# The recurrence's tables in one order for both heads of a pair: corrections in the first 64 rows, values in the last 64

## The chip, the cores and the metric

The kernel runs on one core of one Trainium2 chip. The metric is the device time of one execution in microseconds, taken as the median of several runs.

## What is computed

Two layers of a hybrid trunk over 512 latent and 256 context tokens of width 1024. Each layer projects its normalised input, runs three mixers (differential attention, a two-directional RWKV-7 recurrence, a short convolution), merges them, and ends with a mixture of 16 experts. The change touches the recurrence alone, 8 heads of width 64 in two directions:

```python
def step(s, inp):
    wt, kkt, at, kt, vt = inp[:5]
    sa = jnp.einsum('bhvk,bhk->bhv', s, kkt)
    s = s * wt[:, :, None, :] - sa[..., None] * (kkt * at)[:, :, None, :] + vt[..., None] * kt[:, :, None, :]
    y = jnp.einsum('bhvk,bhk->bhv', s, inp[5]) if emit else None
    return s, y
```

A step decays the state `s`, takes a correction `sa` along the removal key, and adds value times key. The last layer emits nothing for context tokens.

## The kernel before

The recurrence is cut into 12 chunks of 64 tokens (`NCH`), and the 8 heads into 4 pairs, one pair on the 128 partitions: head 0 on rows 0 to 63, head 1 on rows 64 to 127. Both directions stand in the free dimension. So a layer has 48 chain steps, and the kernel 96.

For a chunk, `window` makes what does not depend on the state: decayed keys `kc` (L683, L684) and decayed receptance and removal keys `kr` (L674, L676), their products on TensorE in a bank `slot`, masked by `scc` into `sc` (L700) and `sv` (L701), the keys turned to token order (`tok`, L708), and the inverse of a unit triangular matrix, built in six levels (`nb` L715, `wt` L725, `xt`, `xx`). It is a generator of nine parts. `ahead` advances the windows of the next three chunks by three parts each before a chain step is recorded, so a window is begun three steps ahead and done one step ahead.

`chain` makes what depends on the state: `V` holds the state and the chunk's values; TensorE multiplies it with `sv`, the right-hand side `zr` (L803 to L807) is solved with the inverse, the first solution `sa` (L813) is refined once, the result goes into `V` (L822, L824) and is copied once more to `sa` (L827) where the window emits; the next state is the product with `tok` plus the scaled old state `sf` (L776), added into the next `V` (L844), and the output rows are copied to `y` (L853).

The two heads keep opposite orders. Head 0 has its own corrections and state in rows 0 to 63 and its values in rows 64 to 127, head 1 the other way round:

```python
hs, ho = slice(64 * h, 64 * h + 64), slice(64 - 64 * h, 128 - 64 * h)
v.tensor_tensor(g.sc[hs, :, :nm, hs], ps[hs, :, h, :nm], self.scc[hs, :, :nm], ALU.mult)
v.tensor_tensor(g.sv[ho, :, :nm, h], ps[ho, :, h, :nm], self.scc[ho, :, :nm], ALU.mult)
```

Each instruction on these tables is therefore written once per head, on 64 partitions.

A planner decides when dense work fills in: the input projections and adaLN pieces (`pw`, `pa`) are handed out in small units, a fixed amount per chain step (`fills`: 6.0 per step in the first layer, 3.0 in the second). Weights come by SP's queue; ScalarE rounds them (`w_hi`, L132) and GpSimd takes the rest (`w_lo`, L134). A scheduler orders each engine's instructions when the program is built, by priorities (chain above preparation above windows above dense products). Every engine runs its queue in that order.

Of the kernel before, what the change touches and what calls it, by code (L numbers as in the profile page):

```python
# [8 lines left out]
F32 = mybir.dt.float32  # L9
# [58 lines left out]
class Trunk:  # L68
# [429 lines left out]
    def pair(self, p, full):  # L498
# [48 lines left out]
        def rows(s):  # L547

            self.need(q.u["value"])
            b0, nb = SEGB[s]  # L550
            vt = q.vt[s] = rp.tile([P, 2 * nb, HD], F32, name="vt", tag=f"vt{s}")
            self.requarter(q.v[:, b0 * P:], nb, lambda c, h: vt[64 - 64 * h:128 - 64 * h, c::2])

        def rates(s):

# [4 lines left out]
            if s == 0:  # L560
                q.f = rp.tile([P, 2, NCH], F32, name="f", tag="f", bufs=2)
                q.lm = rp.tile([P, 2, NCH], F32, name="lm", tag="lm")
            nc.gpsimd.memset(D[:, 0, :, 0:1], 0.0)
            nc.gpsimd.memset(D[:, 1, :, 64:65], 0.0)
            for d in range(2):
# [27 lines left out]
            x = slice(max(n0 - 1, 0), n0 + nch - 1)  # L593
            nc.gpsimd.tensor_tensor(q.f[:, :, x], q.f[:, :, x], q.lm[:, :, x.start + 1:x.stop + 1], ALU.add)
            nc.scalar.activation(q.f[:, :, x], q.f[:, :, x], AF.Exp, scale=S_DEC)

        def bonus(s):
            b0, nb = SEGB[s]
# [37 lines left out]
    def window(self, q, n, emit, kb):  # L636
# [28 lines left out]
        t2 = rp.tile(shp, F32, name="t2", tag="t2")  # L665
        pl.tensor_tensor(t2, th, at(e3, True), ALU.mult)


        kc, kr, g.sc = kb
        if emit:  # L670
            self.need(q.u["receptance"])
        for h in range(2):
            hs = slice(64 * h, 64 * h + 64)
            pl.tensor_tensor(kr[hs, :, h, 0], kk[hs], at(e, False)[hs], ALU.mult)  # L674
            if emit:
                pl.tensor_tensor(kr[hs, :, h, 1], two(q.r)[hs], at(e, True)[hs], ALU.mult)  # L676
        yield

        nm = 2 if emit else 1
        g.sv = rp.tile([P, 2, 2, 2, 64], F32, name="sv", tag="sv", bufs=4)  # L680
        for h in range(2):
            hs, ho = slice(64 * h, 64 * h + 64), slice(64 - 64 * h, 128 - 64 * h)
            v.tensor_tensor(kc[hs, :, ho], two(q.k)[hs], t1[hs], ALU.mult)  # L683
            v.tensor_tensor(kc[hs, :, hs], kk[hs], t2[hs], ALU.mult)  # L684
            dst = g.sv[hs, :, :nm, h]
            if n:
                f = q.f[hs, :, n - 1, None, None].to_broadcast([64, 2, nm, 64])
                pl.tensor_tensor(dst, kr[hs, :, h, :nm], f, ALU.mult)
            else:
                pl.tensor_copy(dst, kr[hs, :, h, :nm])  # L690
        yield

        bank = self.slots[n % 3]
        ps = bank.rearrange("p (d h m i) -> p d h m i", d=2, h=2, m=2)
        self.mark()
        for d in range(2):
            self.mm(ps[:, d, :, :nm], kc[:, d], kr[:, d, :, :nm], True, True)
        for h in range(2):
            hs, ho = slice(64 * h, 64 * h + 64), slice(64 - 64 * h, 128 - 64 * h)
            v.tensor_tensor(g.sc[hs, :, :nm, hs], ps[hs, :, h, :nm], self.scc[hs, :, :nm], ALU.mult)  # L700
            v.tensor_tensor(g.sv[ho, :, :nm, h], ps[ho, :, h, :nm], self.scc[ho, :, :nm], ALU.mult)  # L701
        if n < NCH - 1:

            g.tok = rp.tile([P, 2, P], F32, name="tok", tag="tok", bufs=4)
# [6 lines left out]
        i3 = n % 3  # L711
        mat = lambda n_, dt=F16, tag=None, bufs=1: rp.tile([P, 2, P], dt, name=n_, tag=tag or f"{n_}{i3}", bufs=bufs)
        prod = lambda j=0: bank[:, 256 * j:256 * j + 256].rearrange("p (d x) -> p d x", d=2)
        nb = mat("nb")
        nc.gpsimd.tensor_tensor(  # L715
            nb, g.sc[:, :, 0], self.ident[:, None].to_broadcast([P, 2, P]), ALU.add
        )
        x = xt = None
        for l in range(6):
            ps = prod()  # L720
            self.mark()
            for d in range(2):
                self.mm(ps[:, d], nb[:, d], self.ident16 if l == 0 else x[:, d], True, True)
            wt = mat("wt")
            v.tensor_tensor(wt, ps, self.lvm[:, :, l], ALU.mult)  # L725
            if l == 0:
                x = wt
                xt = mat("xt")
                v.tensor_tensor(xt, nb, self.lvm[:, ::-1, 0], ALU.mult)
                yield  # L730
                continue
            ps = prod()
            self.mark()
            for d in range(2):
                self.mm(ps[:, d], wt[:, d], xt[:, d], True, True)
            if l < 5:
                ps2 = prod(1)
                self.mark()
                for d in range(2):
                    self.mm(ps2[:, d], xt[:, d], wt[:, d], True, True)  # L740
                x = mat("xx")
                nc.scalar.activation(x, ps2, AF.Copy)  # L742
                xt = mat("xt")
            else:
                xt = mat("xtr", F32R, "xtr", 4)
            nc.scalar.activation(xt, ps, AF.Copy)
            if l < 5:
                yield
        g.xt = xt

    def value_rows(self, q, n):

        t = self.rp.tile([P, 2, 2, HD], F32, name="V", tag="V", bufs=3)
        s, z0, z1, _ = seg_chunks(n)
        for h in range(2):
            ho = slice(64 - 64 * h, 128 - 64 * h)
            self.nc.gpsimd.tensor_copy(t[ho, :, h], self.two(q.vt[s][ho], z0, z1))
        return t

    def chain(self, q, n, V, emit):  # L760
# [1 line left out]
        nc, rp, tc = self.nc, self.rp, self.tc  # L762
        v = nc.vector
        g = q.win.pop(n)
        halves = [slice(0, 64), slice(64, 128)]
        if n == 0:
            V = self.value_rows(q, 0)
            for h, hs in enumerate(halves):
                nc.gpsimd.memset(V[hs, :, h], 0.0)
        last = n == NCH - 1  # L770
        out = None if last else self.value_rows(q, n + 1)
        if n and not last:
            sf = rp.tile([P, 2, HD], F32, name="sf", tag="sf")
            fc = q.f[:, :, n - 1]
            for h, hs in enumerate(halves):
                nc.gpsimd.tensor_tensor(  # L776
                    sf[hs], V[hs, :, h], fc[hs, :, None].to_broadcast([64, 2, HD]), ALU.mult
                )


        own = list(enumerate(halves))
        both = lambda t, d: t[:, d, None].to_broadcast([P, 2, HD])
        pz = self.psz.tile([P, 512], F32, name="pz", tag="z")
        zz = pz[:, 0:256].rearrange("p (d h x) -> p d h x", d=2, h=2)
        aa = pz[:, 256:384].rearrange("p (d x) -> p d x", d=2)
# [9 lines left out]

        self.mark()
        begin(zz, lambda d: g.sv[:, d, 0])
        sa = first = None
        for it in range(2):
            r = rp.tile([P, 2, HD], F32R, name="zr", tag="zr", bufs=2)  # L800
            for h, hs in own:
                if it:
                    v.tensor_tensor(r[hs], zz[hs, :, h], sa[hs], ALU.subtract)  # L803
                elif h:
                    v.tensor_copy(r[hs], zz[hs, :, h])
                else:
                    nc.scalar.activation(r[hs], zz[hs, :, h], AF.Copy)  # L807
            self.mark()
            for d in range(2):
                self.mma(aa[:, d], g.xt[:, d], r[:, d])  # L810
            if not it:
                sa = rp.tile([P, 2, HD], F32, name="sa", tag="sa", bufs=2)
                nc.scalar.activation(sa, aa, AF.Copy)  # L813
                self.mark()
                for d in range(2):
                    self.mma(zz[:, d], g.sc[:, d, 0], both(sa, d))
                if emit:

                    first = begin(yy, lambda d: g.sv[:, d, 1])
        for h, hs in own:  # L820
            if h:
                nc.scalar.activation(V[hs, :, h], aa[hs], AF.Copy)  # L822
            else:
                v.tensor_copy(V[hs, :, h], aa[hs])  # L824
        if emit:
            sa = rp.tile([P, 2, HD], F32, name="sa", tag="sa", bufs=2)
            nc.scalar.activation(sa, aa, AF.Copy)  # L827
        self.mark()
        tok = lambda d: g.tok[:, d]
        if last:  # L830
# [5 lines left out]
        else:  # L836
            begin(pss, tok)
        if emit:
            for d in range(2):
                self.mma(yy[:, d], g.sc[:, d, 1], both(sa, d))  # L840
        if not last:
            for h, hs in own:
                if n:
                    v.tensor_tensor(out[hs, :, h], pss[hs, :, h], sf[hs], ALU.add)  # L844
                else:
                    v.tensor_copy(out[hs, :, h], pss[hs, :, h])
        if emit:
            s, z0, z1, nch = seg_chunks(n)
            if n % 4 == 0 and n < 8:
# [40 lines left out]
    def rwkv_phase(self, full):  # L890
        nc, tc = self.nc, self.tc
        with ExitStack() as st:
# [2 lines left out]
            self.slots = [psrw.tile([P, 512], F32, name=f"slot{j}") for j in range(3)]  # L895
            self.psmm = st.enter_context(tc.tile_pool(reuse_waits="tile", name="psmm", bufs=1, space=PSUM))
            self.psz = st.enter_context(tc.tile_pool(reuse_waits="tile", name="psz", bufs=1, space=PSUM))
            kc, kr, sc = (
                [self.rp.tile(shape, F32, name=f"{n}{a}") for a in range(m)]
                for n, m, shape in (("kc", 2, [P, 2, P]), ("kr", 2, [P, 2, 2, 2, 64]), ("sc", 4, [P, 2, 2, P]))  # L900
            )
            for t in kr + sc:
                nc.gpsimd.memset(t, 0.0)
            self.mm_bufs, self.fl_tag = {"mm": 1, "fl": 2}, "fl"
            self.units, self.raws, self.ws, self.due = [], [], [], 0.0
# [36 lines left out]
            def ahead(n, steps):  # L942

                for j in range(max(steps)):
                    for a, m in enumerate(steps):
# [1 line left out]
                        if j >= m or n + a >= 4 * NCH:  # L947
                            continue
                        if n + a not in gens:
                            gens[n + a] = self.window(q, c, full or c >= 4, (kc[c % 2], kr[c % 2], sc[(n + a) % 4]))  # L950
                        do(lambda: next(gens[n + a], None))

            call = lambda f, *a: (lambda: f(*a))
# [984 lines left out]
```

## Time and profile before

| what | value |
|---|---|
| median of 3 runs | 3648.34 us (3643.23 to 3650.91) |
| the profiled execution, its time | 3643.64 us |
| its span | 3641.9 us |
| first recurrence, about | 110 to 830 us |
| second recurrence, about | 2110 to 2760 us |

In the profile PE is TensorE's products, PEld its weight loads, DVE VectorE, ACT ScalarE, POOL GpSimd. L81, L85 and L108 are helpers that issue TensorE's instructions, so those are told apart by their tiles. A wait names the instruction that stood idle, then the one that ended it.

### The profile page before, as it was taken

The page shows a single profiled execution, that of the slowest core. Times are in us where ns is not written, and L with a number is a line of the kernel's source. Part 1 is how long each engine was busy: PE and PEld are TensorE (multiplying, and loading weights), DVE is VectorE, ACT ScalarE, POOL GpSimd, SP SyncE. Part 2 cuts the span into 40 slices and gives each one's busy share as a digit, 9 for nine tenths or more (in the row PEclk, how much of TensorE's full clock was granted, in tenths as well). Part 3 has the DMA queues.
Part 4 walks back from the last instruction along what each step waited for, and adds up shares of the span by engine and source line. Part 5 has one row for each costly group of instructions (what it writes and reads, how often), then busy time and mean ns, then how long its engine had stood idle before and what let it go on. Part 6 is the DMA issues. An engine that isn't in the chain of part 4 may idle for free.

```text
span 3641.9 us, 56218 instructions
## 1 busy us (share of the span) xinstructions
PE 3367.1 (92%) x20863; PEld 2243.8 (62%) x20863; DVE 1950.3 (54%) x4725; ACT 1289.5 (35%) x3233; POOL 1133.7 (31%) x1729
## 2 busy tenths in 40 slices
PE   6999999999998989999999898888899989799998
PEld 3777777777987882233333477676678968543342
DVE  6687878764665461121222577878864665412122
ACT  3354555543454211111111345555553542211111
POOL 3555465543320410000000255656554303100000
PEclk9999999999998989999999899999999989899999
DMA  5323132334106336778888410111113154499998
GB/s 182 101 67 98 35 110 67 123 120 144 47 33 222 121 123 253 288 294 327 328 319 335 153 57 29 36 37 39 36 51 101 36 177 157 186 409 409 409 409 350
DMA packets 297045, 620.94 MB, mean 171 GB/s; under 512 B 19258, under 2 KB 160532, under 8 KB 296772
## 3 DMA queue, kind: packets, MB, share of 16 engines
q1 hardware_dynamic: 293028, 605.30, 46.0%
q0 software_dynamic: 1728, 6.29, 0.5%
q10 hardware_dynamic: 2016, 5.77, 0.4%
q8 instruction: 165, 2.70, 0.3%
q14 instruction: 108, 0.88, 0.1%
HBM read 584.00 MB, written 33.29 MB: 170 GB/s over the span
## 4 chain that ended last, share of the span: by engine, by line
PE 50%; DVE 9%; DMA 2%; ACT 2%; issue 2%; POOL 1%; DVEq 0%; ACTq 0%; POOLq 0%
PE ph L81 13%; PE pw L81 6%; PE py L81 6%; PE pc L81 4%; PE po L81 3%; PE slot L81 2%; PE pt L81 2%; PE psc L81 2%; PE pyc L81 2%; PE ba L81 2%; PE pz L85 2%; DMA we<-in_exp_w 2%; PE py L85 1%; PE pxi L81 1%; DVE wt L725 1%
## 5 line engine op out<-in xcount | busy, mean ns | idle before, releaser
L81 PE MATMUL ph<-we,xin 128*64 128x512 f32 x2048 | 513.3, 605 | 5.4 <-DVE hid L1721 2.8
L81 PE MATMUL pw<-hhi,w_hi 128*128 128x512 f32 (+1 forms) x1272 | 490.7, 390 | 15.0 <-ACT w_hi L132 6.7
L81 PE MATMUL pw<-hlo,w_hi 128*128 128x512 f32 (+1 forms) x1272 | 451.2, 359 | 0.0
L81 PE MATMUL pw<-hhi,w_lo 128*128 128x512 f32 (+1 forms) x1272 | 450.9, 360 | 0.3 <-POOL w_lo L134 0.3
L134 POOL TENSOR_TENSOR w_lo<-w_raw,w_hi 128x1024 fp32r<-128x1024 f32 x124 | 300.5, 2429 | 357.2 <-ACT w_hi L132 296.8
L81 PEld LDWEIGHTS ph<-we,xin 128*64 128x64 f32 x2048 | 151.0, 139 | 325.8 <-issue 315.2
L1793 POOL TENSOR_TENSOR ylo<-y,yhi 128x512 fp32r<-128x512 f32 x28 | 35.2, 1281 | 889.3 <-ACT yhi L1792 889.3
L725 DVE TENSOR_TENSOR wt<-slot,lvm 128x256 f16<-128x256 f32 x576 | 230.3, 418 | 94.0 <-PE slot L81 66.1
L81 PEld LDWEIGHTS pw<-hhi,w_hi 128*128 128x128 f32 x1272 | 243.6, 193 | 45.0 <-ACT w_hi L132 8.0
L81 PEld LDWEIGHTS pw<-hhi,w_lo 128*128 128x128 f32 x1272 | 242.1, 192 | 36.1 <-issue 2.6
L81 PEld LDWEIGHTS pw<-hlo,w_hi 128*128 128x128 f32 x1272 | 244.5, 193 | 30.6 <-issue 12.3
L132 ACT ACTIVATE w_hi<-w_raw 128x1024 fp32r<-128x1024 f32 x168 | 177.0, 1057 | 239.7 <-DMA w_raw<-in_w_in 77.8
L81 PE MATMUL py<-we,hT 128*64 128x512 f32 x1024 | 249.3, 607 | 8.3 <-DMA we<-in_exp_w 3.0
L742 ACT ACTIVATE xx<-slot 128x256 f16<-128x256 f32 x384 | 145.9, 382 | 162.8 <-PE slot L81 137.5
L1720 ACT ACTIVATE sl<-ph 64x512 f32<-64x512 f32 x64 | 37.8, 591 | 449.4 <-PE ph L81 429.7
L1803 DVE TENSOR_TENSOR xr<-xr,psc 128x512 f32<-128x512 f32 x144 | 90.4, 681 | 195.5 <-PE psc L81 195.4
L1721 DVE TENSOR_TENSOR hid<-sl,ph 64x512 f32<-64x512 f32 x64 | 44.1, 690 | 268.3 <-ACT sl L1720 267.9
L81 PEld LDWEIGHTS py<-we,hT 128*64 128x64 f32 x1024 | 70.3, 138 | 153.0 <-issue 134.4
L81 PE MATMUL pt<-w_hi,hhi 128*128 128x256 f32 x544 | 155.8, 288 | 5.4 <-ACT xk L1117 2.0
L81 PE MATMUL pt<-w_lo,hhi 128*128 128x256 f32 x544 | 155.5, 286 | 3.4 <-POOL w_lo L134 3.4
L81 PE MATMUL pt<-w_hi,hlo 128*128 128x256 f32 x544 | 154.7, 285 | 0.0
L81 PE MATMUL slot<-xt,wt 128*128 128x128 f16 x960 | 132.2, 224 | 21.6 <-DVE wt L725 21.1
(412 smaller groups left out, 7661.9 us busy)
## 6 DMA issues: line engine op xcount, KB each, us to landing
we<-in_exp_w SPq DMA_DIRECT2D x384, 1024.0 KB
w_raw<-in_w_in SPq DMA_DIRECT2D x124, 512.0 KB
ada_w<-in_ada_w SPq DMA_DIRECT2D x96, 512.0 KB
w_raw<-in_w_branch SPq DMA_DIRECT2D x24, 512.0 KB
w_raw<-in_w_out SPq DMA_DIRECT2D x20, 512.0 KB
gd<-gt SPq DMA_DIRECT2D x24, 384.0 KB
g<-gd SPq DMA_DIRECT2D x24, 384.0 KB
gd<-gt SPq DMA_DIRECT2D x24, 256.0 KB
```

Source lines behind the costliest of these rows:

```text
L81: return self.leg(self.nc.tensor.matmul(out, lhsT, rhs, start=start, stop=stop))
L85: return self.leg(self.nc.tensor.matmul(out, lhsT, rhs, start=start, stop=True, skip_group_check=True))
L132: nc.scalar.activation(hi, raw, AF.Copy)
L134: self.lo_eng.tensor_tensor(lo, raw, hi.bitcast(F32), ALU.subtract)
L725: v.tensor_tensor(wt, ps, self.lvm[:, :, l], ALU.mult)
L742: nc.scalar.activation(x, ps2, AF.Copy)
L1720: nc.scalar.activation(sl, ph[0:64, ns], AF.Silu)
L1721: v.tensor_tensor(hid[0:64, ns], sl, ph[64:128, ns], ALU.mult)
L1793: (v if by_block else self.ylo_eng[nh]).tensor_tensor(lo, yn, hi.bitcast(F32), ALU.subtract)
L1803: v.tensor_tensor(x, x, pt, ALU.add)
```

## The change

Both heads now keep one order: corrections, state and solutions of both heads in rows 0 to 63, with the head in the free dimension, and keys and values in rows 64 to 127. One mask product per window writes `sc` for both heads; GpSimd copies its lower half into the lower half of `sv`. `kc` is written by two products of 128 rows. `nb` is written by two half-height additions into a fixed table whose other blocks were zeroed once. The first solution is evicted by two half-height ScalarE instructions into rows 0 to 63 of a fixed table `x1` whose lower half is zero; the copy of the last solution is gone, and the output's second product takes `V`. `sf` is one GpSimd product with a copy `fs` of the decays. The value rows `vt` are evicted whole, and `value_rows` copies them by direction instead of by head. `sv`, `nb` and `x1` are fixed tables; `sc` comes from a pool of 4; the pool of `xtr` has 3 buffers for 4.

```diff
@@ -548,8 +548,11 @@
 
             self.need(q.u["value"])
             b0, nb = SEGB[s]
-            vt = q.vt[s] = rp.tile([P, 2 * nb, HD], F32, name="vt", tag=f"vt{s}")
-            self.requarter(q.v[:, b0 * P:], nb, lambda c, h: vt[64 - 64 * h:128 - 64 * h, c::2])
+            vt = q.vt[s] = rp.tile([P, nb, 2, HD], F32, name="vt", tag=f"vt{s}")
+            pt = self.bank().rearrange("p (b t) -> p b t", t=P)
+            for b in range(nb):
+                self.tr(pt[:, b], q.v[:, (b0 + b) * P:(b0 + b + 1) * P])
+            nc.scalar.activation(vt.rearrange("p b h x -> p b (h x)"), pt[:, :nb], AF.Copy)
 
         def rates(s):
 
@@ -560,6 +563,7 @@
...
+                q.fs = rp.tile([64, 2, 2, NCH], F32, name="fs", tag="fs", bufs=2)
...
+            for h in range(2):
+                nc.gpsimd.tensor_copy(q.fs[:, h, :, x], q.f[64 * h:64 * h + 64, :, x])
...
-        kc, kr, g.sc = kb
+        kc, kr, g.sv, nb = kb
         if emit:
             self.need(q.u["receptance"])
         for h in range(2):
             hs = slice(64 * h, 64 * h + 64)
-            pl.tensor_tensor(kr[hs, :, h, 0], kk[hs], at(e, False)[hs], ALU.mult)
+            pl.tensor_tensor(kr[hs, :, 0, h], kk[hs], at(e, False)[hs], ALU.mult)
             if emit:
-                pl.tensor_tensor(kr[hs, :, h, 1], two(q.r)[hs], at(e, True)[hs], ALU.mult)
+                pl.tensor_tensor(kr[hs, :, 1, h], two(q.r)[hs], at(e, True)[hs], ALU.mult)
         yield
 
         nm = 2 if emit else 1
-        g.sv = rp.tile([P, 2, 2, 2, 64], F32, name="sv", tag="sv", bufs=4)
+        v.tensor_tensor(kc[:, :, 64:128], two(q.k), t1, ALU.mult)
+        v.tensor_tensor(kc[:, :, 0:64], kk, t2, ALU.mult)
         for h in range(2):
-            hs, ho = slice(64 * h, 64 * h + 64), slice(64 - 64 * h, 128 - 64 * h)
-            v.tensor_tensor(kc[hs, :, ho], two(q.k)[hs], t1[hs], ALU.mult)
-            v.tensor_tensor(kc[hs, :, hs], kk[hs], t2[hs], ALU.mult)
-            dst = g.sv[hs, :, :nm, h]
+            hs = slice(64 * h, 64 * h + 64)
+            dst = g.sv[0:64, :, :nm, h]
             if n:
                 f = q.f[hs, :, n - 1, None, None].to_broadcast([64, 2, nm, 64])
-                pl.tensor_tensor(dst, kr[hs, :, h, :nm], f, ALU.mult)
+                pl.tensor_tensor(dst, kr[hs, :, :nm, h], f, ALU.mult)
             else:
-                pl.tensor_copy(dst, kr[hs, :, h, :nm])
+                pl.tensor_copy(dst, kr[hs, :, :nm, h])
         yield
 
+        g.sc = rp.tile([P, 2, 2, 2, 64], F32, name="sc", tag="sc", bufs=4)
         bank = self.slots[n % 3]
-        ps = bank.rearrange("p (d h m i) -> p d h m i", d=2, h=2, m=2)
+        ps = bank.rearrange("p (d m h i) -> p d m h i", d=2, h=2, m=2)
         self.mark()
         for d in range(2):
-            self.mm(ps[:, d, :, :nm], kc[:, d], kr[:, d, :, :nm], True, True)
-        for h in range(2):
-            hs, ho = slice(64 * h, 64 * h + 64), slice(64 - 64 * h, 128 - 64 * h)
-            v.tensor_tensor(g.sc[hs, :, :nm, hs], ps[hs, :, h, :nm], self.scc[hs, :, :nm], ALU.mult)
-            v.tensor_tensor(g.sv[ho, :, :nm, h], ps[ho, :, h, :nm], self.scc[ho, :, :nm], ALU.mult)
+            self.mm(ps[:, d, :nm], kc[:, d], kr[:, d, :nm], True, True)
+        if emit:
+            fl = lambda t: t.rearrange("p d m h i -> p (d m) h i")
+            mask = self.scc.rearrange("p d m i -> p (d m) i")[:, :, None].to_broadcast([P, 4, 2, 64])
+            v.tensor_tensor(fl(g.sc), fl(ps), mask, ALU.mult)
+        else:
+            mask = self.scc[:, :, 0, None].to_broadcast([P, 2, 2, 64])
+            v.tensor_tensor(g.sc[:, :, 0], ps[:, :, 0], mask, ALU.mult)
+        pl.tensor_copy(g.sv[64:128, :, 0], g.sc[64:128, :, 0])
...
-        nb = mat("nb")
-        nc.gpsimd.tensor_tensor(
-            nb, g.sc[:, :, 0], self.ident[:, None].to_broadcast([P, 2, P]), ALU.add
-        )
+        for h in range(2):
+            hs = slice(64 * h, 64 * h + 64)
+            pl.tensor_tensor(
+                nb[hs, :, hs], g.sc[0:64, :, 0, h], self.ident[0:64, None, 0:64].to_broadcast([64, 2, 64]), ALU.add
+            )
...
     def chain(self, q, n, V, emit):
@@ -762,24 +772,19 @@
         nc, rp, tc = self.nc, self.rp, self.tc
         v = nc.vector
         g = q.win.pop(n)
-        halves = [slice(0, 64), slice(64, 128)]
+        lo = slice(0, 64)
         if n == 0:
             V = self.value_rows(q, 0)
-            for h, hs in enumerate(halves):
-                nc.gpsimd.memset(V[hs, :, h], 0.0)
+            nc.gpsimd.memset(V[lo], 0.0)
         last = n == NCH - 1
         out = None if last else self.value_rows(q, n + 1)
         if n and not last:
-            sf = rp.tile([P, 2, HD], F32, name="sf", tag="sf")
-            fc = q.f[:, :, n - 1]
-            for h, hs in enumerate(halves):
-                nc.gpsimd.tensor_tensor(
-                    sf[hs], V[hs, :, h], fc[hs, :, None].to_broadcast([64, 2, HD]), ALU.mult
-                )
-
-
-        own = list(enumerate(halves))
-        both = lambda t, d: t[:, d, None].to_broadcast([P, 2, HD])
+            sf = rp.tile([64, 2, 2, HD], F32, name="sf", tag="sf")
+            f = q.fs[:, :, :, n - 1].rearrange("p h d -> p d h")[:, :, :, None].to_broadcast([64, 2, 2, HD])
+            nc.gpsimd.tensor_tensor(sf, V[lo], f, ALU.mult)
+
+
+        own = [(0, slice(0, 64)), (1, slice(64, 128))]
...
@@ -795,12 +800,13 @@
 
         self.mark()
         begin(zz, lambda d: g.sv[:, d, 0])
-        sa = first = None
+        x1 = self.x1[n % 2]
+        first = None
         for it in range(2):
             r = rp.tile([P, 2, HD], F32R, name="zr", tag="zr", bufs=2)
             for h, hs in own:
                 if it:
-                    v.tensor_tensor(r[hs], zz[hs, :, h], sa[hs], ALU.subtract)
+                    v.tensor_tensor(r[hs], zz[hs, :, h], x1[lo, :, h], ALU.subtract)
                 elif h:
                     v.tensor_copy(r[hs], zz[hs, :, h])
                 else:
@@ -809,22 +815,19 @@
             for d in range(2):
                 self.mma(aa[:, d], g.xt[:, d], r[:, d])
             if not it:
-                sa = rp.tile([P, 2, HD], F32, name="sa", tag="sa", bufs=2)
-                nc.scalar.activation(sa, aa, AF.Copy)
+                for h, hs in own:
+                    nc.scalar.activation(x1[lo, :, h], aa[hs], AF.Copy)
                 self.mark()
                 for d in range(2):
-                    self.mma(zz[:, d], g.sc[:, d, 0], both(sa, d))
+                    self.mma(zz[:, d], g.sc[:, d, 0], x1[:, d])
...
         for h, hs in own:
             if h:
-                nc.scalar.activation(V[hs, :, h], aa[hs], AF.Copy)
+                nc.scalar.activation(V[lo, :, h], aa[hs], AF.Copy)
             else:
-                v.tensor_copy(V[hs, :, h], aa[hs])
-        if emit:
-            sa = rp.tile([P, 2, HD], F32, name="sa", tag="sa", bufs=2)
-            nc.scalar.activation(sa, aa, AF.Copy)
+                v.tensor_copy(V[lo, :, h], aa[hs])
...
         if emit:
+
             for d in range(2):
-                self.mma(yy[:, d], g.sc[:, d, 1], both(sa, d))
+                self.mma(yy[:, d], g.sc[:, d, 1], V[:, d])
         if not last:
             for h, hs in own:
                 if n:
-                    v.tensor_tensor(out[hs, :, h], pss[hs, :, h], sf[hs], ALU.add)
+                    v.tensor_tensor(out[lo, :, h], pss[hs, :, h], sf[:, :, h], ALU.add)
                 else:
-                    v.tensor_copy(out[hs, :, h], pss[hs, :, h])
+                    v.tensor_copy(out[lo, :, h], pss[hs, :, h])
...
@@ -895,11 +899,13 @@
             self.slots = [psrw.tile([P, 512], F32, name=f"slot{j}") for j in range(3)]
             self.psmm = st.enter_context(tc.tile_pool(reuse_waits="tile", name="psmm", bufs=1, space=PSUM))
             self.psz = st.enter_context(tc.tile_pool(reuse_waits="tile", name="psz", bufs=1, space=PSUM))
-            kc, kr, sc = (
-                [self.rp.tile(shape, F32, name=f"{n}{a}") for a in range(m)]
-                for n, m, shape in (("kc", 2, [P, 2, P]), ("kr", 2, [P, 2, 2, 2, 64]), ("sc", 4, [P, 2, 2, P]))
+            kc, kr, sv, nb, self.x1 = (
+                [self.rp.tile(shape, dt, name=f"{n}{a}") for a in range(m)]
+                for n, m, shape, dt in (
+                    ("kc", 2, [P, 2, P], F32), ("kr", 2, [P, 2, 2, 2, 64], F32), ("sv", 4, [P, 2, 2, 2, 64], F32),
+                    ("nb", 3, [P, 2, P], F16), ("x1", 2, [P, 2, 2, HD], F32))
             )
-            for t in kr + sc:
+            for t in kr + sv + nb + self.x1:
                 nc.gpsimd.memset(t, 0.0)
...
```

The order of the instructions is made anew by the scheduler. On VectorE, in the step before chain step 20 of the first layer, the masks and the state's additions stand so before (`D`, `kk` and `kr_t` are the next pair's preparation, `arow` is adaLN, `cy` the convolution):

```order
L725 TENSOR_TENSOR wt<-slot_581,lvm 128x256
L573 TENSOR_SCALAR D<-D 128x8x64
L844 TENSOR_TENSOR V<-py,sf 64x2x64 x2
L700 TENSOR_TENSOR sc_597<-slot_583,scc 64x4x64
L578 SCALAR_TENSOR_TENSOR D<-scan_469,D 128x520
L725 TENSOR_TENSOR wt<-slot_582,lvm 128x256
L701 TENSOR_TENSOR sv<-slot_583,scc 64x4x64
L700 TENSOR_TENSOR sc_597<-slot_583,scc 64x4x64
L701 TENSOR_TENSOR sv<-slot_583,scc 64x4x64
```

and so after the change:

```order
L735 TENSOR_TENSOR wt<-slot_581,lvm 128x256
L183 TENSOR_TENSOR arow<-pa,arow 128x512
L848 TENSOR_TENSOR V<-py,sf 64x2x64 x2
L706 TENSOR_TENSOR sc<-slot_583,scc 128x512
L545 SCALAR_TENSOR_TENSOR kk<-pk,cols,bk 128x512
L735 TENSOR_TENSOR wt<-slot_582,lvm 128x256
L735 TENSOR_TENSOR wt<-slot_581,lvm 128x256
```

Four masks, between which other work had come, are one; `wt` follows it directly.

A little earlier in the same step the key table is written, before:

```order
L582 TENSOR_SCALAR a<-a 128x512
L683 TENSOR_TENSOR kc_591<-pk,t_5967 64x2x64
L684 TENSOR_TENSOR kc_591<-kk,t_5970 64x2x64
L824 COPY V<-pz 64x2x64
L683 TENSOR_TENSOR kc_591<-pk,t_5967 64x2x64
L684 TENSOR_TENSOR kc_591<-kk,t_5970 64x2x64
```

and after:

```order
L685 TENSOR_TENSOR kc_591<-pk,t_5812 128x2x64
L686 TENSOR_TENSOR kc_591<-kk,t_5815 128x2x64
L120 SCALAR_TENSOR_TENSOR kr_t<-kr_t,kss 128x8
L1034 TENSOR_TENSOR cy<-cy,pw 128x256
L830 COPY V<-pz 64x2x64
```

Two products stand where four stood, and the preparation of the next pair (`kr_t`, L120) comes in between.

On GpSimd, in a step of the same stretch, before:

```order
L757 COPY V<-vt 64x2x64 x2
L776 TENSOR_TENSOR sf<-V,f 64x128 x2
L715 TENSOR_TENSOR nb<-sc_594,ident 128x256
L688 TENSOR_TENSOR sv<-kr_593,f 64x4x64 x2
L666 TENSOR_TENSOR t_6400<-a,e_6394 128x128
L664 TENSOR_TENSOR t_6397<-t_6397,e_6394 128x128
```

and after:

```order
L767 COPY V<-vt 64x128 x2
L784 TENSOR_TENSOR sf<-V,fs 64x256
L725 TENSOR_TENSOR nb_599<-sc,ident 64x2x64 x2
L710 COPY sv_596<-sc 64x2x128
L692 TENSOR_TENSOR sv_597<-kr_593,f 64x4x64
```

`sf` is one instruction, `nb` two, and the copy of `sc` into `sv` stands between `nb` and the scaled keys.

## Rows read from the trace of the kernel before

**Rows 1.** The page, busy time, share of the span and instructions of each engine.

```profile
PE 3367.1 (92%) x20863; PEld 2243.8 (62%) x20863; DVE 1950.3 (54%) x4725; ACT 1289.5 (35%) x3233; POOL 1133.7 (31%) x1729
```

**Rows 2.** Both recurrences and the second's first half: busy by engine (count), granted clock, DMA, GB/s.

```profile
110.00:830.00 720.00, 686.18 (x5015) 546.98 (x5013) 547.36 (x1426) 364.37 (x1074) 381.54 (x690) 0.99 0.28 91
2110.00:2760.00 650.00, 585.19 (x4002) 451.23 (x4000) 491.96 (x1312) 344.49 (x1009) 375.38 (x672) 0.97 0.14 42
2110.00:2435.00 325.00, 292.56 (x1938) 225.60 (x1936) 252.97 (x664) 167.46 (x484) 193.33 (x345) 0.95 0.13 38
```

**Rows 3.** TensorE's waits over the whole span: total us, times, longest us.

```profile
PE slot L81 <- DVE wt L725: 22.1, 29, 2.4
...
PE pz L85 <- DVE V L844: 19.6, 38, 1.0
...
PE slot L108 <- DVE sv L701: 10.2, 21, 1.1
...
PE pz L85 <- DVE zr L805: 8.2, 7, 3.3
...
PE pz L85 <- DVE zr L803: 5.2, 8, 2.8
```

**Rows 4.** VectorE's groups, shapes apart: count, busy us, mean ns, idle before them.

```profile
L684 DVE TENSOR_TENSOR kc<-kk,t 64x128 f32<-64x128 f32 x192 | 78.6, 409 | 5.9 <-POOL t L666 5.4
L683 DVE TENSOR_TENSOR kc<-pk,t 64x128 f32<-64x128 f32 x192 | 78.3, 408 | 16.1 <-PE slot L108 9.6 <-POOL t L664 3.5 <-PE slot L81 0.7
L701 DVE TENSOR_TENSOR sv<-slot,scc 64x256 f32<-64x256 f32 x160 | 67.4, 421 | 3.3
L700 DVE TENSOR_TENSOR sc<-slot,scc 64x256 f32<-64x256 f32 x160 | 67.0, 419 | 8.2 <-PE slot L81 5.5
...
L701 DVE TENSOR_TENSOR sv<-slot,scc 64x128 f32<-64x128 f32 x32 | 9.2, 289 | 0.7
L700 DVE TENSOR_TENSOR sc<-slot,scc 64x128 f32<-64x128 f32 x32 | 9.1, 285 | 2.3 <-PE slot L81 2.0
...
L634 DVE COPY vt<-rq 64x256 f32<-64x256 f32 x16 | 6.8, 423 | 2.5 <-ACT vt L632 1.1 <-POOL V L757 1.0
```

**Rows 5.** VectorE's full-height products from PSUM, the same view.

```profile
L615 DVE TENSOR_TENSOR bv<-bk,pv 128x512 f32<-128x512 f32 x8 | 5.5, 684 | 4.5 <-PE bk L81 4.4
...
L615 DVE TENSOR_TENSOR bv<-bk,pv 128x256 f32<-128x256 f32 x4 | 1.7, 414 | 0.2 <-PE bk L81 0.2
```

**Rows 6.** The key table's writes: instructions, min/median/max ns, first and last start.

```profile
L684 DVE TENSOR_TENSOR kc<-kk,t x192: 272/284/2472, 98.5 to 2698.9; 64x128 f32<-64x128 f32 x192
```

**Rows 7.** Timeline from 2424 us: start, us, engine, instruction, idle before it.

```profile
2423.83 2.96 DVE L684 TENSOR_TENSOR kc<-kk,t 64x128 f32<-64x128 f32 x2
...
2424.23 2.42 POOL L134 TENSOR_TENSOR w_lo<-w_raw,w_hi 128x1024 fp32r<-128x1024 f32 x1
...
2427.69 0.62 PE L85 MATMUL pz<-zr,xtr 128*128 128x64 f32 x2 [1.97 <-DVE zr L805]
```

**Rows 8.** ScalarE's evictions in the chain, shapes apart.

```profile
L813 ACT ACTIVATE sa<-pz 128x128 f32<-128x128 f32 x96 | 27.3, 284 | 25.2 <-PE pz L85 24.7 <-DVE wt L725 0.3
L822 ACT ACTIVATE V<-pz 64x128 f32<-64x128 f32 x96 | 26.2, 273 | 47.2 <-DVE V L824 45.0
...
L827 ACT ACTIVATE sa<-pz 128x128 f32<-128x128 f32 x80 | 22.2, 278 | 1.9
```

**Rows 9.** GpSimd's groups that are removed, joined or nearest in price.

```profile
L688 POOL TENSOR_TENSOR sv<-kr,f 64x256 f32<-64x256 f32 x152 | 100.6, 662 | 26.2 <-PE py L85 19.2 <-PE pz L85 0.2
...
L715 POOL TENSOR_TENSOR nb<-sc,ident 128x256 f16<-128x256 f32 x96 | 76.0, 792 | 50.6 <-DVE sc L700 48.8
L676 POOL TENSOR_TENSOR kr<-pr,e 64x128 f32<-64x128 f32 x160 | 68.0, 425 | 8.2 <-ACT e L651 3.1 <-PE slot L81 2.9 <-DVE kr_t L119 1.4
L776 POOL TENSOR_TENSOR sf<-V,f 64x128 f32<-64x128 f32 x160 | 68.0, 425 | 64.7 <-DVE V L844 58.0 <-DVE V L846 1.3
...
L690 POOL COPY sv<-kr 64x256 f32<-64x256 f32 x8 | 3.8, 472 | 1.1 <-PE py L85 0.9
```

More of the change, by code (lines that the diff above doesn't have):

```diff
@@ L744, in window @@
             else:
-                xt = mat("xtr", F32R, "xtr", 4)
+                xt = mat("xtr", F32R, "xtr", 3)
             nc.scalar.activation(xt, ps, AF.Copy)
@@ L753, in value_rows @@
         t = self.rp.tile([P, 2, 2, HD], F32, name="V", tag="V", bufs=3)
[L754 to L757, printed above, removed]
+        s, *z, _ = seg_chunks(n)
+        for d in range(2):
+            c = 64 * (z[d] % 2)
+            self.nc.gpsimd.tensor_copy(t[64:128, d], q.vt[s][c:c + 64, z[d] // 2])
         return t
@@ L949, in ahead @@
                         if n + a not in gens:
-                            gens[n + a] = self.window(q, c, full or c >= 4, (kc[c % 2], kr[c % 2], sc[(n + a) % 4]))
+                            gens[n + a] = self.window(q, c, full or c >= 4, (kc[c % 2], kr[c % 2], sv[(n + a) % 4], nb[c % 3]))
                         do(lambda: next(gens[n + a], None))
```

## The prediction

> **What bounds the kernel now.** I read the page's busy line first. TensorE is busy for 92% of the span and VectorE for 54% [rows 1], but these are averages, and the change touches only the two recurrences. So the second view is the table of stretches. The first recurrence (110 to 830 us) has TensorE at 686 of 720 us and VectorE at 547; the second (2110 to 2760 us) has TensorE at 585 of 650 us and VectorE at 492 [rows 2]. TensorE therefore stands still for 720 - 686.2 = 33.8 us in the first and 650 - 585.2 = 64.8 us in the second, 98.6 us together, and VectorE is at 1039 of 1370 us, 76%. The count of TensorE's instructions and their sizes stay as they are (below), so these 98.6 us, and whatever a higher granted clock gives, are all that the change can win. The clock was 0.99 in the first recurrence, 0.97 in the second and 0.95 in the second's first half [rows 2].
>
> The third view says who ends TensorE's standstills. Five pairs of the recurrence, all ended by VectorE, make 22.1 + 19.6 + 10.2 + 8.2 + 5.2 = 65.3 us [rows 3], two thirds of the 98.6. They are not alike. `slot <- DVE wt` is the solve, waiting for a masked product that stands in VectorE's queue behind other work. `slot <- DVE sv` is the transposition of the key table, which overwrites the bank that the four masking instructions read, and so waits for the last of the four. `pz <- DVE V` is the next chain step waiting for the new state, 0.5 us each time: mostly the bare duration of the two additions. `pz <- DVE zr` is the chain's right-hand side, again behind a queue.
>
> **The change, part by part.**
>
> *Masks.* Four half-height products per window become one full-height one. Now: 67.4 + 67.0 us for the 80 windows that emit, 9.2 + 9.1 us for the other 16 [rows 4], 152.7 us in all. Then: a full-height product of 512 columns from PSUM took 684 ns and one of 256 columns 414 ns [rows 5]; the half-height one of 256 columns takes 419 to 421 ns [rows 4], so the height costs nothing. 80 x 0.684 + 16 x 0.414 = 61.3 us. VectorE loses 91 us. In one window the last mask ends 4 x 0.42 - 0.68 = 1.0 us earlier.
>
> *Key table.* Four half-height products become two full-height ones: 78.6 + 78.3 = 156.9 us now [rows 4], half of it then, if each keeps its mean: -78 us. The ends: the median is 284 ns [rows 6] against the mean of 409, so 384 x 0.284 = 109 us is work and 48 us is blockage. If all the blockage stays, the saving is 192 x 0.284 = 55 us; if all goes, 156.9 - 55 = 102 us. I take the middle, since fewer instructions stand in its way for less time.
>
> What the blockage is, the timeline shows: two key products took 2.96 us while GpSimd's `w_lo` took 2.42 us beside them, and TensorE then stood still for 1.97 us for a right-hand side queued behind them [rows 7]. The Trainium skill (SBUF — State Buffer, section "SBUF: two separate sides") says that a VectorE instruction with two SBUF inputs and a GpSimd one that reads SBUF take a shared pair of ports as an exclusive lock, so that the later one waits for the whole of the other. This case's rows agree with it (the longest key product is 2472 ns [rows 6]). By that rule the blockage would not be halved, since the next two-input product would wait in place of the missing ones; the sum below would lose about 2 us.
>
> *Value rows.* VectorE's two evictions per segment go: 6.8 us [rows 4] and 16 shorter ones at about 0.29, together some 11 us. One full-height ScalarE eviction replaces ScalarE's two; off the path.
>
> VectorE in all: -91 - 78 - 11 = -180 us, from 1039 to 859 of the 1370 us: 76% becomes 63%.
>
> *Chain on ScalarE.* The first solution is now moved by two half-height evictions (273 ns, as `V` [rows 8]) instead of one of 284 ns, and the copy of the last solution (22.2 us in all) goes: 192 x 0.273 - 27.3 - 22.2 = +2.9 us of work. On the path the second half comes 0.26 us later in each of 96 chain steps. Bounds: 0, and 96 x 0.26 = 25 us. No wait of TensorE for `sa` is among the large ones [rows 3], because planned dense products stand in between; I take 2 us. Nothing else on ScalarE waits long behind it.
>
> *GpSimd.* Added: 96 copies of 64x256 at 472 ns = 45 us; the identity addition as two instructions, 192 x 0.425 - 76.0 = +6 us; 32 tiny copies, some 6 us. Joined: the state's scaling, 80 x 0.662 instead of 68.0 = -15 us [rows 9]. Sum +42 us on 757: 55% becomes 58%. Behind the added copy stand the scaled keys of the next window and the products for the window after; the copied rows are wanted only when the chain reaches that window, two steps later. `nb` stands before the copy. No pair with GpSimd is in the large waits [rows 3]. I cost it at nothing; without that cover it is up to 42 us.
>
> *TensorE.* The built program has 19,645 TensorE instructions before and after, of the same sizes. Zeros in the fixed tables are multiplied like anything else. Cost nothing.
>
> **The sum.** *sv*, 10.2 us: its longest wait is 1.1 us and the mean 0.5, and the mask now ends 1.0 us earlier: -9. *wt*, 22.1 us: the part that is queue shrinks with the load; taking queueing as load / (1 - load), 0.76 gives 3.2 and 0.63 gives 1.7, so nearly half: -10. *zr*, 13.4 us: the same with some that waits for other long work (normalisation, convolution): -5. *V*, 19.6 us: bare duration; -3. ScalarE +2. That is -25. The granted clock of the second's first half was 0.95 where the denser first recurrence had 0.99 [rows 2]: at most 4% of 325 us = 13 us; a third of it, -4. Sum **-29 us**. The profiled execution took 3643.64 us (span 3641.9 and 1.7 around it), so 3614.6 on its scale; it lies 4.7 below the median of the runs shown, 3648.34, and on that scale I forecast **3619 us**. A difference of 0.2%, 7.3 us, is about what a measurement can tell from none.
>
> **Rivals.**
>
> *More than that (0.17).* The wait for V shrinks too, and `wt` nearly goes. For it: all five pairs end at VectorE. All of 65.3 us would give 3583; three quarters, 49 us, plus the clock's 13 give 3586; I put this case at 3590 to 3604. Against it: V is a latency of two additions that stay.
>
> *No change (0.17).* The order of each queue is fixed when the program is built, and dense products are placed among the chain's. A wait removed at one place is then met at the next product, which is late for another reason (ScalarE's `xx`, the 6 to 7 dense products in front). In the first recurrence TensorE is at 95% already. It would give 3641 to 3655.
>
> *GpSimd takes the place (0.13).* The solve of a window starts with `nb`, now two instructions, and each window's GpSimd work is 42 / 96 = 0.44 us longer, in a queue that is blocked for 2.4 us at a time by `w_lo`. If the solve follows that queue, 96 x 0.44 = 42 us come in, and half of VectorE's gain (14 us) is not met: +28 us, 3676. It decides once `nb` ends after TensorE has run through the dense products placed ahead of the solve. Against it: GpSimd is at 55% and no pair with it is large.
>
> *The change does not do what it says.* The built program has 512 VectorE instructions less (4195 for 4707), so this has no chance worth a number.
>
> **How the numbers follow.** Forecast, -8 to -43 us (3605 to 3640): 0.53. More: 0.17. None: 0.17. Slower: 0.13. Faster by over 0.2% has 0.53 + 0.17 = 0.70. The range takes in the forecast's bounds, the larger part of the stronger case and the lower two thirds of no change: 3592 to 3651.
>
> **What would show it.** VectorE's busy time in the recurrences falls by about 180 us; `slot <- DVE sv` (then `sc`) nearly vanishes from TensorE's waits; `wt` halves; TensorE's idle time falls from 99 to about 70 us; GpSimd grows by some 40 us. Wrong would be: VectorE falls as said, but TensorE's idle stays and other releasers take the waits; or GpSimd's `nb` appears before the solve; or the stretches outside the recurrences move by more than some us, since the order is made anew there too.

## The result and the profile after

The changed kernel takes 3594.22 us (median of 4, 3591.06 to 3597.41) against 3647.66 us for the kernel before (4 runs, 3643.23 to 3650.91): a ratio of 0.9862, 95% interval 0.985 to 0.9873. That is 53 us less, on the forecast side and nearly twice the 29 us of the sum. It lies inside the range of 3592 to 3651 us, 2 us from its lower end.

The page's busy line of the changed kernel, against [rows 1]:

```profile
PE 3351.7 (93%) x20863; PEld 2237.3 (62%) x20863; DVE 1799.5 (50%) x4213; ACT 1295.1 (36%) x3233; POOL 1202.4 (33%) x1875
```

TensorE's instructions are as many, VectorE's are 512 fewer. VectorE is 151 us less busy, GpSimd 69 us more, ScalarE 6 us more.

To see where the time went, the recurrences are cut at their own first and last chain step. Of the kernel before (us, then busy time of TensorE, its weight loads, VectorE, ScalarE, GpSimd, each with its count, the granted clock as a share of the higher of TensorE's two levels, 2.4 and 1.2 GHz, DMA share, GB/s):

```profile
117.00:843.90 726.90, 689.83 (x5031) 550.41 (x5029) 543.05 (x1420) 365.95 (x1077) 379.71 (x677) 0.99 0.29 94
2137.10:2739.80 602.70, 538.19 (x3775) 413.78 (x3774) 471.62 (x1262) 326.56 (x975) 349.05 (x637) 0.97 0.13 40
```

and of the changed kernel:

```profile
117.00:828.30 711.30, 680.51 (x5033) 545.85 (x5032) 466.08 (x1176) 367.39 (x1069) 409.12 (x744) 0.99 0.29 95
2127.80:2693.10 565.30, 522.41 (x3770) 407.13 (x3770) 403.88 (x1019) 330.80 (x983) 383.69 (x705) 0.98 0.14 42
```

The first recurrence is 15.6 us shorter, the second 37.4, together 53.0. The stretch between them gives 6.3 us back (843.9 to 2137.1 before, 828.3 to 2127.8 after), and the profiled executions differ by 46.4 us; that the two recurrences give the same number as the medians is a coincidence. TensorE's idle time in the two falls from 37.1 + 64.5 = 101.6 us to 30.8 + 42.9 = 73.7: 27.9 us. The rest of these 53.0, 25.1 us, is **busy** time, from 1228.0 to 1202.9 us, with the same products (8806 and 8803 records). The profile models where a product ends, so the border between idle and busy is less certain than their sum.

TensorE's waits of the changed kernel, against [rows 3] (total us, times, longest us):

```profile
PE slot L81 <- DVE wt L735: 26.0, 23, 4.6
...
PE py L85 <- ACT V L828: 6.7, 11, 1.9
...
PE pz L85 <- DVE zr L809: 4.4, 7, 2.2
...
PE pz L85 <- DVE zr L811: 3.6, 9, 0.7
...
PE slot L108 <- DVE sc L706: 3.3, 2, 2.5
...
PE pz L85 <- DVE V L848: 0.5, 2, 0.3
```

`wt` has not shrunk (22.1 before), `zr` has (13.4 to 8.0), the transposition's wait for the mask too (10.2 to 3.3), and the wait for the new state `V`, 19.6 us before, is down to 0.5. These five pairs fall from 65.3 us to 37.8, nearly all of the 27.9 us of idle time. The groups that answer to [rows 4], [rows 6], [rows 8] and [rows 9], first VectorE's:

```profile
L706 DVE TENSOR_TENSOR sc<-slot,scc 128x512 f32<-128x512 f32 x80 | 55.3, 691 | 7.3 <-PE slot L81 4.9 <-PE py L85 0.5
...
L686 DVE TENSOR_TENSOR kc<-kk,t 128x128 f32<-128x128 f32 x96 | 46.6, 486 | 5.7 <-POOL t L672 5.6
...
L685 DVE TENSOR_TENSOR kc<-pk,t 128x128 f32<-128x128 f32 x96 | 44.6, 465 | 18.9 <-PE slot L108 16.3 <-POOL t L670 1.5 <-POOL nb L725 0.3
...
L709 DVE TENSOR_TENSOR sc<-slot,scc 128x256 f32<-128x256 f32 x16 | 6.7, 421 | 1.4 <-PE slot L81 1.1
```

GpSimd's:

```profile
L725 POOL TENSOR_TENSOR nb<-sc,ident 64x128 f16<-64x128 f32 x192 | 96.1, 501 | 15.8 <-DVE sc L706 6.7 <-DVE sc L709 1.3
...
L784 POOL TENSOR_TENSOR sf<-V,fs 64x256 f32<-64x256 f32 x80 | 51.0, 637 | 16.0 <-DVE V L848 11.1 <-DVE kr_t L120 0.3
L710 POOL COPY sv<-sc 64x256 f32<-64x256 f32 x96 | 47.4, 494 | 5.7
```

and ScalarE's first solution:

```profile
L819 ACT ACTIVATE x<-pz 64x128 f32<-64x128 f32 x192 | 51.8, 270 | 25.0 <-PE pz L85 22.3 <-DVE wt L735 1.4
```

The masks cost 62.0 us (61.3 in the sum). The key table costs 91.2, where 78.5 were taken: its saving is 66 us, not 78.

### The profile page after: what moved, and what is told of

Read it like the earlier page. It is cut to its first block, busy times and chain, and to the rows that moved or that the text cites. A ratio compares the mean times of both kernels' runs of the same rounds, so it can differ in the third digit from the quotient of the medians.

```text
span 3595.5 us, 55785 instructions
## 1 busy us (share of the span) xinstructions
PE 3351.7 (93%) x20863; PEld 2237.3 (62%) x20863; DVE 1799.5 (50%) x4213; ACT 1295.1 (36%) x3233; POOL 1202.4 (33%) x1875
## 5 line engine op out<-in xcount | busy, mean ns | idle before, releaser
L134 POOL TENSOR_TENSOR w_lo<-w_raw,w_hi 128x1024 fp32r<-128x1024 f32 x124 | 298.3, 2412 | 345.7 <-ACT w_hi L132 276.5
L1726 ACT ACTIVATE sl<-ph 64x512 f32<-64x512 f32 x64 | 37.8, 591 | 449.2 <-PE ph L81 429.5
```

What stands on the lines that cost most here:

```text
L134: self.lo_eng.tensor_tensor(lo, raw, hi.bitcast(F32), ALU.subtract)
L1726: nc.scalar.activation(sl, ph[0:64, ns], AF.Silu)
```

## The experiments

All have the changed kernel as their base unless they say otherwise. The kernel before ran beside each group; its medians were 3649.8, 3648.2 and 3646.1 us. The changed kernel's 3594.2 us stands beside 3647.7 us, so a few us of each difference from it can be drift between the groups.

**What happened to `V`.** One chain step of the kernel before: the end of the chain (start, us, engine, instruction, idle before it).

```profile
411.14 0.27 DVE L824 COPY V<-pz 64x128 f32<-64x128 f32 x1
...
411.75 0.28 ACT L827 ACTIVATE sa<-pz 128x128 f32<-128x128 f32 x1
...
411.78 0.71 PE L85 MATMUL py<-V,tok 128*128 128x128 f32 x4
...
413.74 0.61 PE L85 MATMUL py<-sa,sc 128*128 128x128 f32 x4
...
414.60 0.58 DVE L844 TENSOR_TENSOR V<-py,sf 64x128 f32<-64x128 f32 x2
```

A step of the changed kernel:

```profile
397.82 0.27 DVE L830 COPY V<-pz 64x128 f32<-64x128 f32 x1
398.13 0.28 ACT L828 ACTIVATE V<-pz 64x128 f32<-64x128 f32 x1 [0.59 <-DVE V L830]
...
398.74 0.66 PE L85 MATMUL py<-V,tok 128*128 128x128 f32 x4
...
399.24 0.61 PE L85 MATMUL py<-V,sc 128*128 128x128 f32 x4
...
399.89 0.59 DVE L848 TENSOR_TENSOR V<-py,sf 64x128 f32<-64x128 f32 x2
```

The state's addition is recorded behind the output's second product, which shares its bank, and starts after it. Before, that product took the copy `sa` and stood in TensorE's queue 1.25 us behind the state's product; now it takes `V` and follows at once. From the end of the state's product the addition came 2.11 us later before (412.49 to 414.60) and 0.49 us later after (399.40 to 399.89); over the 80 steps with such an addition the medians are 1.5 and 0.5 us. So the wait for V was not the bare duration of two additions. Hence two theories: W, that this is what the sum missed, and L, that VectorE's load does it all. Four kernels tell them apart.

*e1: the copy put back.*

```diff
+        if emit:
+            nc.scalar.activation(x1[lo], V[lo], AF.Copy)
...
-                self.mma(yy[:, d], g.sc[:, d, 1], V[:, d])
+                self.mma(yy[:, d], g.sc[:, d, 1], x1[:, d])
```

> The changed kernel with one part undone: where a window emits, ScalarE again copies the last solution (one instruction of 64x256 into the fixed table x1) and the output's second product takes that copy. The chunk's own values are left out of the output rows (the table's lower half is zero); no instruction less for it. Theory W (the state's addition waits for the output's products in the same bank, and these for ScalarE's copy): the addition again starts 1 us or more after the state's product, TensorE's waits for V come back (some 20 us), the time is 3594 + 25 to 35 = 3619 to 3629 us. Theory L (VectorE's load alone): within 6 us of 3594.

Measured: 3628.1 us (ratio to before 0.9945, 0.9932 to 0.9957), 34 us over the changed kernel, as W has it. The addition again starts 1.4 us (median) after the state's product, and the wait is back:

```profile
PE pz L85 <- DVE V L850: 14.5, 35, 0.8
```

The copy takes 413 ns here, against 278 [rows 8]: 33.1 us in all.

*e2: the kernel before, the state's additions recorded ahead of the output's second product* (two blocks of `chain` change places).

> The kernel before, with the state's additions recorded ahead of the output's second product and nothing else changed. Theory W: the additions start about 0.5 us after the state's product instead of 1.7, TensorE's waits for V fall from 24 to below 6 us, and the time is 3648 - 20 to 30 = 3618 to 3628 us. Theory L: VectorE's load is as before, so 3641 to 3655 us.

Measured: 3661.1 us (1.0027, 1.0015 to 1.0038), slower than before, although the additions now start within 0.1 us (median) of the state's product. W falls here. TensorE's waits in this run:

```profile
PE slot L81 <- DVE wt L725: 35.9, 35, 3.0
...
PE pz L85 <- DVE zr L803: 11.6, 19, 2.1
...
PE pz L85 <- DVE zr L805: 7.4, 7, 2.3
...
PE pz L85 <- DVE V L841: 4.2, 9, 0.9
...
PE pz L85 <- DVE V L843: 2.6, 4, 0.8
```

The wait for V is down from 24 to 6.8 us, about as expected, and `wt` (22.1 before) and `zr` (13.4) have grown by 19 us together. A wait that a row names is not time that one gets by removing it: here as much came back in the waits for other VectorE products.

*e3: VectorE's saving undone.*

```diff
+            v.tensor_tensor(kc[hs, :, 64:128], two(q.k)[hs], t1[hs], ALU.mult)
+            v.tensor_tensor(kc[hs, :, 0:64], kk[hs], t2[hs], ALU.mult)
...
+        for h in range(2):
+            for r in range(2):
+                hs = slice(64 * r, 64 * r + 64)
+                v.tensor_tensor(g.sc[hs, :, :nm, h], ps[hs, :, :nm, h], self.scc[hs, :, :nm], ALU.mult)
```

> The changed kernel with VectorE's saving undone: the masks in four half-height products and the key table in four, as many and as long as before (some +170 us of VectorE). Theory W: the copy stays away, so about half of the gain stays: 3610 to 3625 us. Theory L: the whole gain goes, 3640 to 3655 us.

Measured: 3666.9 us (1.0047, 1.0033 to 1.0061): 73 us over the changed kernel and 17 over the kernel before. The whole gain goes and more, even past what L expected. Without VectorE's saving the new order gains nothing.

*e4: the changed kernel with the state's additions first.*

> The changed kernel with the state's additions recorded ahead of the output's second product. Theory W: the addition still follows the output's products by their own 0.45 us, so up to 80 x 0.45 = 36 us of latency go, of which TensorE's idle time shows a part: 3580 to 3592 us. Theory L: within 6 us of 3594.

Measured: 3593.3 us, against 3594.2: L's figure. Here too the additions start within 0.1 us (median) of the state's product. Starting them earlier, as such, gains nothing in either kernel.

**The load or the place?** Each half of the saving alone, and as much VectorE work that nobody waits for.

*e9: four half-height masks. e10: four half-height key products* (the two parts of e3's edit). *e11: a sum that nothing reads:*

```diff
+        junk = rp.tile([P, 2, 3], F32, name="junk", tag="junk")
+        v.tensor_reduce(junk, self.lvm[:, :, 0:3], axis=AX.X, op=ALU.add)
```

> The changed kernel with only the masks undone: four half-height products per window, +91 us of VectorE. Theory Q (VectorE's queue as a whole: each microsecond of it costs about 0.4 us of the kernel, wherever it stands): 3594 + 35 to 45 us. Theory P (the place: the masks are what the transposition and the solve wait for): 3594 + 55 to 75 us, most of what masks and key table cost together (73 us).

> The changed kernel with only the key table undone: four half-height products, +65 to 80 us of VectorE. Theory Q: 3594 + 25 to 35 us. Theory P: 3594 + 0 to 15 us, since the key table is written two steps ahead.

> The changed kernel with one sum over 768 elements per partition added per window on VectorE, right behind the mask, into a scratch tile that nothing reads: some 0.95 us each, 96 times, +91 us, as much as the masks' saving. Theory Q: as much as the masks cost, 3594 + 35 to 45 us. Theory P: nothing waits for it, 3594 + 0 to 12 us.

Measured: e9 3620.4 us, +26; e10 3637.6 us, +43; e11 3624.2 us, +30. VectorE's group of e11:

```profile
L712 DVE TENSOR_REDUCE junk<-lvm 128x6 f32<-128x768 f16 x96 | 90.9, 947 | 2.6 <-POOL hlo L438 1.4
```

91 us of work for nobody costs as much as the 91 us of the masks, to within what the order alone does (below). So that other work waits for the masks has no price of its own that shows; their load in the queue has one. The price is 0.29 to 0.33 us per us, below what Q expected. That the place in the queue does not matter is not shown: e11's sum stands where the masks stand. The key products stand elsewhere and are dearer: +43 for +75 us of products (166.7 us in e10, 91.2 in the changed kernel), 0.57 per us, above what either theory expected. e9 and e10 add up to 70, about e3's 73.

*e6: GpSimd's copy made twice.*

> The changed kernel with GpSimd's copy of the masked products made twice: +47 us of GpSimd. If GpSimd is covered, as the prediction has it: 3588 to 3600 us. If its queue decides anything (the rival in which GpSimd takes the place): 3594 + 20 to 40 us.

Measured: 3603.8 us, +10: between the two expectations. The second copies add 41 us (88.6 in all, against 47.4). But +10 us is no more than the order alone does (below), so no price of GpSimd's load is shown, nor that it has none.

*e7: the first of the two solution evictions on VectorE.*

> The changed kernel with the first of the two evictions of the first solution on VectorE, so that both run at once: 96 instructions of some 275 ns move from ScalarE to VectorE, +26 us of it. If the two in a row on ScalarE cost what the prediction took (2 us): VectorE's load outweighs it, 3594 + 3 to 10 us. If they lay fully on the path (25 us): 3594 - 10 to 20 us.

Measured: 3615.8 us, +22. The two evictions in a row on ScalarE do not show as a cost; the move costs 13 us more than its 26 us of load would at e11's rate, 9 us.

**Why are the key products dearer?** Theory R: ScalarE and GpSimd prepare `t1` in one buffer and stand until the last key product has read it. In e12, e13 and e14 it has two (`bufs=2`), in e10's kernel, in the changed one and in the one before.

> As e10_keys (four half-height key products), and t1, the table that ScalarE and GpSimd prepare for them, has two buffers instead of one. Theory R (what the keys cost beyond their load is ScalarE standing at t1 until the last key product has read the old one, 60 us in all there, with the solve's evictions queued behind): the wait goes from 60 to below 10 us, and the time falls from 3638 to 3594 + 15 to 30 = 3609 to 3624 us. Theory Q (load alone, the rest is the order's chance): 3630 to 3645 us, as without it.

> The changed kernel with two buffers for t1 and nothing else. Theory R: ScalarE's wait for the key products (25 us) goes, 3580 to 3590 us. Theory Q: 3588 to 3600 us.

> The kernel before with two buffers for t1 and nothing else. Theory R: ScalarE's wait for the key products (53 us) goes, and with it 15 to 30 us of the kernel: 3618 to 3633 us. Theory Q: 3641 to 3655 us.

Measured: 3647.1 us (9 over e10), 3609.1 (15 over the changed kernel), 3654.5 (8 over the kernel before). All are slower, and the wait did not go: in e13 it is 17.9 us (24.6 in the changed kernel), in e14 51.0 (52.9 before). In e10 and then in e12 it reads:

```profile
ACT t L666 <- DVE kc L687: 59.6, 57, 3.6
```

```profile
ACT t L666 <- DVE kc L687: 53.4, 50, 3.8
```

So the second buffer did not take the wait away, and R is neither shown nor excluded. What the three do show is how far the order alone can move the time: a buffer that leaves the work as it is and changes this wait by 2 to 7 us, but has the scheduler make a new order, moves it by 8 to 15 us. (All three are slower, so a cost of the second buffer itself is not excluded.) That much has to be allowed in every difference here, the change's own 53 us included; e2's +11, e6's +10 and what e7 costs beyond its load lie within it, e1, e3, e9, e10 and e11 do not.

None of the twelve beats the changed kernel clearly; e4 equals it. The prices do not add up to the change: the copy put back (34 us) and VectorE's saving undone (73) make 107 us, twice the gain. The change brought costs as well, such as GpSimd's 69 us of work, and no run undoes both parts at once.

## Why the prediction was right, and where it was too small

- *Bound.* Half right: the gain lies in the two recurrences, and none of it in the count of products. But the standstills and a higher clock were to be "all that the change can win". The standstills gave 27.9 of the 53.0 us; the other 25.1 came out of busy time, and the clock makes only about a third of those (below).
- *Masks.* 62.0 us for 61.3. Right. e9 prices their return at 26 us.
- *Key table.* "I take the middle" of the blockage was too good: 96 products at 486 and 96 at 465 ns leave 91.2 - 192 x 0.284 = 36.7 of the 48 us. The Trainium skill (SBUF — State Buffer, section "SBUF: two separate sides") states an exclusive lock; what the prediction drew from it, that the blockage would not be halved, is the nearer one.
- *VectorE in all.* In the recurrences it fell by 145 us (1014.7 to 870.0), not 180, and from 76% to 68% of the time, not 63%. The key table makes 12 us of the difference. Another product with two SBUF operands, `xt` from `nb` and `lvm`, grew from 38.0 to 48.5 us; over the experiments it takes between 35.9 and 56.4 (54.4 in e10, with all key products back), so its growth is not tied to the number of key products.
- *GpSimd.* +69 us, not +42: `nb` in two parts costs 96.1 us for 81.6. That this load costs nothing is neither shown nor refuted by e6. The rival with GpSimd did not happen: no pair with it is large.
- *ScalarE.* 51.8 us for 52.4. The removed copy was counted as work alone. It also held the output's product and, behind that, the state's addition; e1 prices it at 34 us in the changed kernel. e2 and e4 show that this is not the wait for V by itself. Nor is it that the output's product comes late: in e4 it starts 2.3 us (median) behind the state's product, later than in e1 (0.9), and costs nothing. A rival that no run tests is the copy's own 33 us on ScalarE; e1 with the additions first would tell. So what the removed copy paid for stays open.
- *V: "bare duration; -3".* Wrong: 19.6 us went almost whole. But e2 shows that a row taken away so may come back in others.
- *`wt`: "nearly half: -10".* Wrong: 22.1 became 26.0. That a wait goes as load / (1 - load) was assumed, and no run shows it: VectorE's load fell and this wait did not. Too much here and too little at V cancelled by luck, and idle time fell by 27.9 us where the terms for VectorE made 27. The other two terms held: `sv` -6.9 us for -9, `zr` -5.4 for -5.
- *The mis-sized term* is the clock's -4, the only one that let busy time shrink: it shrank by 25.1 us. Two parts of that can be estimated from the traces. The granted clock, averaged to a third digit, went from 0.986 to 0.990 in the first recurrence and from 0.966 to 0.976 in the second; on their busy time that is 3 + 5 = 8 us, twice the term. (Over the whole kernel it is 0.963 both times; in the stretch between the recurrences it went from 0.96 to 0.95.) And products overlap in a dense stream, as these two of the kernel before do:

```profile
410.50 0.28 PE L81 MATMUL pw<-hhi,w_lo 128*128 128x256 f32 x1
...
410.62 0.28 PE L81 MATMUL pw<-hhi,w_hi 128*128 128x256 f32 x1
```

Each takes 0.28 us and the next begins after 0.12, so at a standstill some 0.16 us of the last product overlap nothing. TensorE stood still 215 times in the two recurrences before and 152 times after: 63 x 0.16 = 10 us. The other 7 us stay open. None of this was tested by a run of its own, but the runs show busy time rising and falling with idle time: in the second recurrence e3 stands idle 73.4 and is busy 544.6 us, the kernel before 64.5 and 538.2, the changed one 42.9 and 522.4, with the same products.

```profile
2142.90:2760.90 618.00, 544.56 (x3768) 416.71 (x3767) 476.22 (x1250) 333.26 (x983) 375.33 (x704) 0.95 0.13 39
```

(e3's second recurrence, columns as above; its granted clock is 0.95.) The Trainium skill (Trainium Kernel Development and Optimization, section "Performance Expectations") calls the busy time of products a bad measure of how close a kernel is to its roofline, the bound that the hardware sets, since they are pipelined; the trace agrees, with 0.28 us of busy time begun every 0.12 us.

The case that came about is the rival "more than that", at 3590 to 3604 us, which had 0.17. Half of its mechanism came true: the wait for V went, and `wt` did not. It had 49 us of standstills and 13 of clock; the runs show 28 of standstills and some 8 of clock, so that its time came out, too, is partly luck.

## What to carry to other kernels

Where an engine at some 70% feeds a nearly full TensorE through in-order queues, its load has a price even where nothing waits for it: here 0.3 us of time per us, as a sum read by nobody showed, and for the key products nearly twice that. Named waits tell where the lateness surfaces, not what their removal pays; and TensorE's idle time was here about half of what went with it. Where a scheduler makes the order anew, first measure how far a change that should do nothing moves the time: 8 to 15 us here.

## What was not expected of the hardware

VectorE products of 128 rows with two SBUF operands kept a mean of 465 to 486 ns where the 64-row ones had 409, at nearly the same least duration (277 and 272 ns): the longest was 2441 ns, about one GpSimd `w_lo` of 2412 ns. Half as many of them kept three quarters of the blockage.
